# A hybrid encoder layer: state fetches moved a step forward, bias rows spread head by head, transposes at the top, and another row buffer

## The chip, the cores and the metric

The kernel runs on one core of a Trainium2 chip. The metric is the device time of one execution in microseconds, as the median of several runs. A core has five engines with queues of their own: TensorE (PE; its weight loads are listed as PEld), VectorE (DVE), ScalarE (ACT), GpSimd (POOL) and SyncE (SP). SP computes nothing here; it issues most of the transfers. Some transfers of results are issued on ACT's queue. Each queue is worked off in order, and an instruction that waits holds up those behind it on its engine.

## The reference

One layer of a hybrid encoder, for a prompt of 2048 rows and for a sample of 8 streams of 16 rows, all in float32 with a model width of 1024:

```python
h = rms_norm(x, norm_g[0]); z = h @ w_in                  # 1024 -> 3592, columns split among heads
att = band_attention(qa, ka, va, rel_table)               # 8 heads of 64, own 64-row chunk + 8 before, clipped relative bias
hb, (c1, n1, m1) = mlstm_sequence(qb, kb, vb, ig, lf, ..) # 4 heads of 128, matrix memory c, gates, running maximum
mix = concat(rms_norm(att), headnorm(hb) * g_mlstm * sigmoid(ob)) @ w_out
x = x + rms_norm(mix, norm_g[1])
u = rms_norm(x, norm_g[2]) @ w_up                         # 1024 -> 2 * 2816
y = b_conv + sum(ext[:, j:j + S] * w_conv[j] for j in range(3))   # causal, along the rows
x = x + rms_norm((gelu(gate) * up) @ w_down, norm_g[3])
```

For the sample, attention also reads a cache of 512 keys and values per stream, the mLSTM starts from given states (`state_c`, one matrix of 128 x 129 for each of 4 heads and 8 streams, the normaliser in its first column), and the convolution has its own two rows of history. Besides both outputs the layer returns new keys, values, states and convolution histories.

## The kernel before

**Precision.** Each float32 operand of a large product is split into a high and a low part, and a product is made of three matmuls (`mm3`, L93 to L97): high by high, high by low, low by high. The split is a cast on ACT and a subtraction on DVE.

**Part one, projection with attention and mLSTM** (about 0 to 1200 us). The rows are taken in two halves, and in each half 14 groups of columns of `w_in` follow one another: for each group TensorE multiplies the transposed, normed rows with the group's weights, which arrive in raw tiles `wi_raw` (L1155) and are split at L1161 and L1162. `norm_tile` (L209) norms 128 rows and turns them with eight transposes into `hT`. Two other streams of work run between these matmuls, each as a `Pipe` (L135): attention (`att_stream`) and the mLSTM (`mem_stream`). A pipe holds small generators, "units". Each call of `step` takes a new unit from its source and moves every unit in it on by one `yield`; a unit's first stage usually issues its loads, the next splits, the next multiplies. `pump` (L171) steps the two pipes in turn, by a running estimate of TensorE and DVE time that each `yield` carries.

**The order of the queues.** The program text gives the priorities. A planner then simulates all the engines and takes, whenever one is free, the earliest instruction of the program that could run, so a load may be put ahead of others that stand before it, as far as its buffer is free. A transfer inside `tc.keep_in_program_order` keeps its place. The order so found is fixed in the queues.

**The bias.** The attention bias depends on the distance of query and key alone. `build_bias` (L285) loads the reversed table (`near`, L290), negates it and fills the far side (L292, L293), writes both to a DRAM row `ext` of 767 numbers for each head, and then copies each head's row 128 times to `relrow` (L298, 383.5 KB a head). `load_head` (L315) reads a 128 x 640 tile `nb` out of `relrow` with rows one shorter than the step, which gives the diagonal pattern. Its unit is the first of the attention pipe. On the other pipe run, at the same time, `prep_sample` and `prep_prompt` (L541), which make the stabilised gates: cumulated sums, a running maximum `cm` (a scan on DVE at L548), transposes `rt`, `mp` and `pkT`, exponentials on ACT (L570 to L573).

**The sample's states.** `mlstm_sample` handles one head for the eight streams. Its units are `own`, four `batches` (L759) of two streams each, and `finish`. A batch loads two states into `cs` (L763), makes masked queries and values (POOL and DVE), multiplies (L775, L776), updates the states (L779, L780) and stores them (L781). `cs` shares two buffers, tag `num`, with the results of the prompt's mLSTM chunks, which `finish_heads` stores at L649.

**Part two, output projection** (`project`, L956, to about 1340 us), with the third part's rows being prepared beside it.

**Part three, the FFN** (to the end). It takes the rows in three blocks of about 700. For a block, the normed rows are turned and combined into seven operands `B[0]` to `B[6]` of a Strassen-like scheme (`h2_units`, L1051; one tile each, 128 x 2 x 4 x 384). For each of 22 column groups the up projection runs seven products, the convolution makes `y` rows on ACT and DVE, and the gated result `g` is stored to DRAM in `gd`. Then the down projection reads `gd` back, tile by tile (`fetch`, L1438, with the load at L1447), splits it and multiplies. While it runs, the next block's `h2_units` are stepped. `row` (L1044) hands out the 128 x 1024 row tiles of tag `yq`, three buffers: they hold `y` and `g` in the up projection, the fetched `gr` in the down projection, the rows `x2r` of the first block, and the squares `sq`, an output nobody reads, which ACT writes at L1069 while it sums them.

Of the kernel before, what the change touches and what calls it, by code (L numbers as in the profile page):

```python
# [44 lines left out]
def hymba_step(ctx: ExitStack, tc: tile.TileContext, I: dict, O: dict):  # L45
# [27 lines left out]
    make_identity(nc, ident)  # L73
    nhalf = const.tile([P, 8], F32, name="nhalf")
    nc.vector.memset(nhalf, -0.5)

    def mean_square(ms, ssq, n, eps=EPS):
        nc.gpsimd.tensor_scalar(ms, ssq, 1.0 / n, eps, op0=ALU.mult, op1=ALU.add)
# [203 lines left out]
    def raw_tile(name):  # L282
        return pa.tile([P, LS], F32, tag="raw", name=name, bufs=3)

    def build_bias():  # L285
        ext = dt_([HA, SQ], "ext")

        def unit():
            far, near = raw_tile("relf")[:HA, :383], raw_tile("reln")[:HA, :SQ - 383]
            tc.keep_in_program_order(nc.sync.dma_start(near, I["rel_rev"][:, 0:SQ - 383]))  # L290
            yield 0.0, 0.0
            nc.vector.tensor_scalar(near, near, -1.0, None, op0=ALU.mult)  # L292
            nc.vector.tensor_copy(far, near[:, 0:1].broadcast_to([HA, 383]))  # L293
            nc.sync.dma_start(ext[:, 383:SQ], near)
            nc.sync.dma_start(ext[:, 0:383], far)
            yield 0.0, 0.75
            for h in range(HA):
                nc.sync.dma_start(relrow[h], ext[h:h + 1, :].broadcast_to([P, SQ]))  # L298
                yield 0.0, 0.0

        yield unit()
        yield FLUSH
# [12 lines left out]
    def load_head(s):  # L315
        pair, kg, hh, h, nm = s.pair, s.kg, s.hh, s.h, s.nm
        if kg % 2 == 0:
            nb = pa.tile([P, 640], F32, tag="nb", name=f"nb{nm}", bufs=2)
            nc.sync.dma_start(nb, bias_src(h, P, 640))
            nc.gpsimd.memset(nb[0:64, 576:640], BIG)  # L320
            nc.gpsimd.memset(nb[64:128, 0:64], BIG)
            nbs[hh] = nb
        s.nb = nbs[hh]
        rows = slice(hh * 64, hh * 64 + 64)
        qr = raw_tile(f"qraw{nm}")[:, :512]
        krs = [raw_tile(f"kraw{nm}_{g}")[:, :512] for g in s.segs]
        for r in range(2):
            nc.sync.dma_start(qr[r * 64:r * 64 + 64, :], qTd[pair][kg][rows, :])
        for kr, g in zip(krs, s.segs):
            for r in range(2):  # L330
                nc.sync.dma_start(kr[r * 64:r * 64 + 64, :], kTd[pair][g][rows, :])
        yield 0.0, 0.0
        s.kh = pa.tile([P, 1024], F32R, tag="kh", name=f"kh{nm}", bufs=2)
        s.kl = pa.tile([P, 1024], F32R, tag="kl", name=f"kl{nm}", bufs=2)
        s.qs = pa.tile([P, 512], F32R, tag="qs", name=f"qs{nm}", bufs=2)
        nc.scalar.copy(s.qs, qr)
        nc.vector.tensor_tensor(s.qs[64:128], qr[64:128], s.qs[64:128], op=ALU.subtract)
        for si, kr in enumerate(krs):
            c = slice(si * 512, (si + 1) * 512)
            nc.scalar.copy(s.kh[:, c], kr)  # L340
            nc.vector.tensor_tensor(s.kl[:, c], kr, s.kh[:, c], op=ALU.subtract)
        new = [g for g in s.segs if g == kg or (h, g) not in vhl]
        vrs = [raw_tile(f"vraw{nm}_{g}")[:, :4 * DA].rearrange("p (a d) -> p a d", a=4) for g in new]
        for vr, g in zip(vrs, new):
            nc.sync.dma_start(vr, vd[h // 4][g][:, :, (h % 4) * DA:(h % 4 + 1) * DA])
        yield 0.0, 0.6 + 0.6 * len(krs)
        for vr, g in zip(vrs, new):
            t = pa.tile([P, 4, P], F32R, tag="vhl", name=f"vhl{nm}_{g}", bufs=4)
            nc.scalar.copy(t[:, :, 0:DA], vr)
            nc.vector.tensor_tensor(t[:, :, DA:P], vr, t[:, :, 0:DA], op=ALU.subtract)  # L350
            vhl[h, g] = t
        s.v = {g: vhl[h, g] for g in s.segs}
        if kg % 2:
            for g in s.segs:
                vhl.pop((h, g))
        yield 0.0, 0.34 * len(new)
# [294 lines left out]
    def mlstm(h, half):  # L651
# [22 lines left out]
        def chunk(s, c):  # L674
            cc = 2 * s.pc + c
            r = cc * HB + h
            col = lambda i: cols[:, i, r:r + 1]
            q_, k_ = s.qk[:, 0, c * P:(c + 1) * P], s.qk[:, 1, c * P:(c + 1) * P]
            sp = ps_sm(f"ms{s.nm}_{c}")
            nc.tensor.matmul(sp[:, 0:P], k_, q_, start=True, stop=True)  # L680
            transpose(sp[:, P:2 * P], k_)
            w = pm.tile([P, P], F32, tag="wexp", name=f"w{s.nm}_{c}", bufs=2)
            nc.scalar.activation(w, s.mb[:, c, :], AF.Exp, bias=col(0), scale=-1.0)
            kw = pm.tile([P, P], F32, tag="kw", name=f"kw{s.nm}_{c}", bufs=2)
            nc.scalar.activation(kw, sp[:, P:2 * P], AF.Identity, scale=col(3))
            nc.vector.tensor_tensor(w, sp[:, 0:P], w, op=ALU.mult)
            yield 0.32, 0.2
            if c == 0:
                s.num = pm.tile([P, 2, e], F32, tag="num", name=f"num{s.nm}", bufs=2)
            num = s.num  # L690
            acc = ps_sm(f"ma{s.nm}_{c}")
            nc.tensor.matmul(acc[:, e:2 * e], q_, cst[h], start=True, stop=True)
            nc.tensor.matmul(acc[:, 0:e], w, s.va[:, c, :], start=True, stop=True)
            nc.tensor.matmul(acc[:, 2 * e:3 * e], kw, s.va[:, c, :], start=True, stop=True)
            nc.vector.scalar_tensor_tensor(cst[h], cst[h], dec[:, cc, h:h + 1], acc[:, 2 * e:3 * e],
                                           op0=ALU.mult, op1=ALU.add)
            nc.scalar.activation(num[:, c, :], acc[:, e:2 * e], AF.Identity, scale=col(1))
            nc.vector.tensor_tensor(num[:, c, :], num[:, c, :], acc[:, 0:e], op=ALU.add)
            yield 0.65, 0.47
            if c == 0:  # L700
                return
            r0 = 2 * s.pc * HB + h
            sg, o = s.t0 // 4, s.t0 % 4
            finish_heads(num, cols[:, 2, r0:r0 + HB + 1:HB], s.og, h, 2,
                         mixd[sg][:, o:o + 2, 512 + h * DH:512 + (h + 1) * DH], s.nm)
            if half == 1 and s.pc == 3:
                nc.sync.dma_start(O["c_prompt"][h], cst[h])
            yield 0.0, 1.3
# [11 lines left out]
    def mlstm_sample(h):  # L720
# [36 lines left out]
            yield 0.2, 0.2  # L757

        def batches(bp):  # L759
            yield 0.0, 0.0  # L760
            bs = slice(2 * bp, 2 * bp + 2)
            cs = pm.tile([P, 2, e], F32, tag="num", name=f"cs{h}_{bp}", bufs=2)
            nc.sync.dma_start(cs, I["state_c"][h][:, bs])  # L763
            qz = pm.tile([P, 2, P], F32, tag="mqk", name=f"qz{h}_{bp}", bufs=2)
            nc.gpsimd.memset(qz, 0.0)
            for i in range(2):
                c = slice((2 * bp + i) * DS, (2 * bp + i + 1) * DS)
                nc.gpsimd.tensor_copy(qz[:, i, c], s.qt[:, c])
            vz = pm.tile([P, 2, e], F32, tag="mvo", name=f"vz{h}_{bp}", bufs=2)
            nc.vector.tensor_tensor(vz, s.va.unsqueeze(1).broadcast_to([P, 2, e]),  # L770
                                    ind[:, bs].unsqueeze(2).broadcast_to([P, 2, e]), op=ALU.mult)
            yield 0.0, 0.3
            cu = ps_sm(f"cu{nm}_{bp}")
            for i in range(2):
                nc.tensor.matmul(cu[:, 2 * e:3 * e], qz[:, i, :], cs[:, i, :], start=(i == 0), stop=(i == 1))  # L775
            nc.tensor.matmul(cu[:, :2 * e], s.kw, vz.rearrange("p b e -> p (b e)"), start=True, stop=True)  # L776
            nc.vector.scalar_tensor_tensor(s.num[:, 0, :], cu[:, 2 * e:3 * e], col(1), s.num[:, 0, :],
                                           op0=ALU.mult, op1=ALU.add)
            nc.vector.tensor_tensor(cs, cs, dec[:, h, bs].unsqueeze(2).broadcast_to([P, 2, e]), op=ALU.mult)  # L779
            nc.vector.tensor_tensor(cs, cs, cu[:, :2 * e].rearrange("p (b e) -> p b e", b=2), op=ALU.add)  # L780
            nc.sync.dma_start(O["c_sample"][h][:, bs], cs)  # L781
            yield 0.85, 0.8
# [259 lines left out]
        return ffn.p3.tile([P, 512], F32, tag="q", name=name, bufs=11)  # L1042

    def row(name):  # L1044
        return ffn.p3.tile([P, D], F32, tag="yq", name=name, bufs=3)

    def new_B(i, b):
        pool = ffn.p3 if i < EARLY_B else ffn.p4
# [2 lines left out]
    def h2_units(b, between=()):  # L1051
# [3 lines left out]
        def unit(halves, col, n, nm):  # L1055
# [10 lines left out]
            rs = {}  # L1066
            for t, x in rows_.items():
                ssq = small.tile([P, 1], F32, tag="ssq", name=f"fssq{t}")
                nc.scalar.activation(row(f"sq{t}"), x, AF.Square, accum_out=ssq)  # L1069
                rs[t] = rsqrt_mean(ssq, D, f"n2_{t}")  # L1070
            yield 0.0, 0.0
            for t, x in rows_.items():
# [606 lines left out]
```

## Time and profile before

| | |
|---|---|
| median of 3 runs | 2814.91 us |
| lowest, highest | 2813.02, 2816.5 us |
| the profiled execution | 2812.18 us |
| its span, first to last instruction | 2810.5 us |
| mean granted TensorE clock | 0.997 |

A line of a timeline is: start in us, length in us, engine, line of the kernel, operation, what it writes and reads, and in brackets how long the engine had been idle and what ended the idle time. SPq and ACTq are transfers as their queue issues them; the length is that of the issue, not of the transfer. A line of the waits is: who waited, for whom, total us, times, longest. A line of the windows gives the busy time of each engine in one stretch, then the clock that TensorE was granted there, the share in which the DMA engines were busy, and GB/s.

### The profile page before, as it was taken

The numbers are of one execution on the slowest core, as the hardware profiler recorded it, in microseconds if no ns is written. First come the engines' busy times: TensorE is split into PE (matmuls) and PEld (weight loads), VectorE is DVE, ScalarE is ACT, GpSimd is POOL, SyncE is SP. The second block draws the span as 40 slices with busy tenths as digits, with TensorE's granted clock in tenths as the row PEclk, the third lists the DMA queues.
The fourth block names the chain that finished last, engine by engine and source line by source line (L and its number), as shares of the span: only waits on it lengthen the run. The fifth ranks groups of instructions, "written<-read, shape, count | busy, mean of one in ns | idle before, by whom it ended". The sixth has DMA issues, their size and how long they took to land.

```text
span 2810.5 us, 47049 instructions
## 1 busy us (share of the span) xinstructions
PE 2729.8 (97%) x16587; PEld 2550.2 (91%) x16587; DVE 1871.9 (67%) x3442; ACT 1407.5 (50%) x2836; POOL 446.2 (16%) x876
## 2 busy tenths in 40 slices
PE   8899999999999999999999999999999999999998
PEld 7899999998899998878999988799999878999887
DVE  5344455646446678666989886457878854888855
ACT  4345545644356666543545555445555543555533
POOL 1000010211100003244221110011111310222221
PEclk9999999999999999999999999999999999999999
DMA  4544355557555455355645455644544775555585
GB/s 164 170 128 125 111 155 156 177 148 215 164 173 148 141 177 172 106 180 203 199 160 173 162 177 172 218 145 154 157 154 139 266 264 155 171 181 175 188 298 197
DMA packets 313418, 486.04 MB, mean 173 GB/s; under 512 B 55426, under 2 KB 150622, under 8 KB 313054
## 3 DMA queue, kind: packets, MB, share of 16 engines
q1 hardware_dynamic: 274590, 449.21, 50.9%
q10 hardware_dynamic: 38592, 33.83, 3.6%
q8 instruction: 130, 2.13, 0.3%
q14 instruction: 106, 0.87, 0.1%
HBM read 359.36 MB, written 126.70 MB: 173 GB/s over the span
## 4 chain that ended last, share of the span: by engine, by line
PE 51%; DVE 5%; DMA 2%; issue 2%; ACT 1%; POOL 1%; SPq 0%; DVEq 0%; POOLq 0%; ACTq 0%
PE uec L95 5%; PE uec L96 5%; PE uec L97 5%; PE dn L96 4%; PE dn L97 4%; PE dn L95 4%; PE ua L97 3%; PE ua L96 3%; PE ua L95 3%; PE dnm L95 2%; PE dnm L97 2%; PE dnm L96 2%; PE wo L95 1%; PE wo L97 1%; PE wo L96 1%
## 5 line engine op out<-in xcount | busy, mean ns | idle before, releaser
L95 PE MATMUL uec<-B,wuh 128*128 128x384 f32 (+1 forms) x720 | 236.3, 329 | 6.9 <-DVE uu L1492 6.1
L96 PE MATMUL uec<-B,wuh 128*128 128x384 f32 (+1 forms) x720 | 235.2, 327 | 0.0
L97 PE MATMUL uec<-B,wul 128*128 128x384 f32 (+1 forms) x720 | 233.3, 327 | 0.0
L1251 DVE TENSOR_TENSOR gl<-gr,gh 128x768 fp32r<-128x768 f32 (+3 forms) x141 | 118.7, 849 | 163.3 <-ACT gh L1250 163.0
L1250 ACT CAST gh<-gr 128x768 fp32r<-128x768 f32 (+3 forms) x141 | 102.1, 736 | 219.1 <-PE dn L96 194.1
L1250 ACT CAST wuh<-wu 128x512 fp32r<-128x512 f32 x255 | 141.7, 617 | 91.2 <-PE uec L96 87.5
L95 PE MATMUL dn<-wdh,gh 128*128 128x512 f32 x466 | 182.9, 392 | 2.5 <-DVE ug L1403 2.5
L96 PE MATMUL dn<-wdl,gh 128*128 128x512 f32 x466 | 183.9, 395 | 0.0
L97 PE MATMUL dn<-wdh,gl 128*128 128x512 f32 x466 | 168.4, 396 | 0.0
L1251 DVE TENSOR_TENSOR wul<-wu,wuh 128x512 fp32r<-128x512 f32 x255 | 164.3, 683 | 2.8 <-DMA x2d<-mx 2.8
L96 PE MATMUL vo<-wi_l,hT 128*128 128x256 f32 x544 | 155.7, 286 | 0.0
L95 PE MATMUL vo<-wi_h,hT 128*128 128x256 f32 x544 | 154.9, 285 | 0.6 <-DVE mt L199 0.6
L97 PE MATMUL vo<-wi_h,hT 128*128 128x256 f32 x544 | 155.3, 285 | 0.0
L387 DVE CUSTOM_DVE_ANT_0 tmp<-s,nb 128x640 f32<-128x640 f32 (+4 forms) x128 | 94.3, 737 | 77.8 <-PE s L377 74.3
L95 PEld LDWEIGHTS uec<-B,wuh 128*128 128x128 f32 x720 | 135.1, 188 | 11.1 <-DVE uu L1492 8.1
L96 PEld LDWEIGHTS uec<-B,wuh 128*128 128x128 f32 x720 | 135.2, 188 | 0.1
L97 PEld LDWEIGHTS uec<-B,wul 128*128 128x128 f32 x720 | 135.0, 188 | 0.0
L388 ACT ACTIVATE tmp<-tmp,mn 128x640 f32<-128x640 f32 (+4 forms) x128 | 97.6, 762 | 69.9 <-DVE mn L387 65.6
L95 PE MATMUL qk<-hT,wi_h 128*128 128x384 f32 (+1 forms) x384 | 128.6, 335 | 3.5 <-ACT qk_st L226 1.7
L400 DVE TENSOR_TENSOR ptl<-pt,pth 128x640 fp32r<-128x640 f32 (+4 forms) x128 | 93.5, 737 | 55.4 <-ACT pth L399 54.4
L97 PE MATMUL qk<-hT,wi_l 128*128 128x384 f32 (+1 forms) x384 | 128.0, 333 | 0.0
L96 PE MATMUL qk<-hT,wi_h 128*128 128x384 f32 (+1 forms) x384 | 127.8, 333 | 0.0
(409 smaller groups left out, 8886.6 us busy)
## 6 DMA issues: line engine op xcount, KB each, us to landing
wu<-in_w_up SPq DMA_DIRECT2D x220, 256.0 KB, 4.0
wu<-wsd SPq DMA_DIRECT2D x176, 256.0 KB, 3.7
wdr<-in_w_down SPq DMA_DIRECT2D x132, 256.0 KB, 5.4
gr<-gd SPq DMA_DIRECT2D x78, 384.0 KB, 3.9
wi_raw<-in_w_in SPq DMA_DIRECT2D x52, 512.0 KB, 4.3
wsd<-ws SPq DMA_DIRECT2D x88, 256.0 KB, 4.0
gd<-g SPq DMA_DIRECT2D x44, 384.0 KB, 2.7
kraw<-kTd SPq DMA_DIRECT2D x112, 128.0 KB, 3.2
```

The costliest lines, as they stand in the source:

```text
L95: nc.tensor.matmul(out, ah, bh, start=start, stop=False, skip_group_check=onto)
L96: nc.tensor.matmul(out, ah, bl, start=False, stop=False, skip_group_check=onto)
L97: nc.tensor.matmul(out, al, bh, start=False, stop=stop, skip_group_check=onto)
L387: nc.vector.tensor_tensor_reduce(o_, s_, b_, 1.0, 3e38, ALU.add, ALU.min, accum_out=mn)
L388: nc.scalar.activation(tmp[:, :n], tmp[:, :n], AF.Exp, bias=mn, scale=-1.0, accum_out=rsum[:, i % 4, hh:hh + 1])
L400: nc.vector.tensor_tensor(s.ptl[:, sl, qc], ptv, s.pth[:, sl, qc], op=ALU.subtract)
L1250: nc.scalar.copy(h, r)
L1251: nc.vector.tensor_tensor(l, r, h, op=ALU.subtract)
```

## The change

Five edits:

1. At the top, 28 transposes of the identity matrix into a PSUM tile that nothing reads.
2. `build_bias` lets three more steps pass between the load of the table and its use. It spreads the rows of heads 0 and 1 alone. The row of head h + 2 is spread when head h is loaded for the first time, and these copies keep their place in the program.
3. `batches` allocates and loads `cs` ahead of its first `yield` in place of behind it, and the tag `num` gets a third buffer.
4. The squares of full 128-row tiles go into the part of `B[0]` that the same unit overwrites two stages later; those of the half tiles of the last block still go to a row tile.
5. The tag `yq` gets a fourth buffer.

```diff
+    warm = ps_sm("warm")
+    for _ in range(28):
+        transpose(warm[:, :P], ident)
...
+    ext = dt_([HA, SQ], "ext")
+
+    def spread_bias(h):
+        tc.keep_in_program_order(nc.sync.dma_start(relrow[h], ext[h:h + 1, :].broadcast_to([P, SQ])))
+
     def build_bias():
-        ext = dt_([HA, SQ], "ext")
 
         def unit():
             far, near = raw_tile("relf")[:HA, :383], raw_tile("reln")[:HA, :SQ - 383]
             tc.keep_in_program_order(nc.sync.dma_start(near, I["rel_rev"][:, 0:SQ - 383]))
-            yield 0.0, 0.0
+            for _ in range(4):
+                yield 0.0, 0.0
...
-            for h in range(HA):
-                nc.sync.dma_start(relrow[h], ext[h:h + 1, :].broadcast_to([P, SQ]))
+            for h in range(2):
+                spread_bias(h)
                 yield 0.0, 0.0
...
             vhl[h, g] = t
+        if s.kg == 0 and h + 2 < HA:
+            spread_bias(h + 2)
...
-                s.num = pm.tile([P, 2, e], F32, tag="num", name=f"num{s.nm}", bufs=2)
+                s.num = pm.tile([P, 2, e], F32, tag="num", name=f"num{s.nm}", bufs=3)
...
         def batches(bp):
+            bs = slice(2 * bp, 2 * bp + 2)
+            cs = pm.tile([P, 2, e], F32, tag="num", name=f"cs{h}_{bp}", bufs=3)
+            nc.sync.dma_start(cs, I["state_c"][h][:, bs])
             yield 0.0, 0.0
-            bs = slice(2 * bp, 2 * bp + 2)
-            cs = pm.tile([P, 2, e], F32, tag="num", name=f"cs{h}_{bp}", bufs=2)
-            nc.sync.dma_start(cs, I["state_c"][h][:, bs])
...
     def row(name):
-        return ffn.p3.tile([P, D], F32, tag="yq", name=name, bufs=3)
+        return ffn.p3.tile([P, D], F32, tag="yq", name=name, bufs=4)
...
                 ssq = small.tile([P, 1], F32, tag="ssq", name=f"fssq{t}")
-                nc.scalar.activation(row(f"sq{t}"), x, AF.Square, accum_out=ssq)
+                if n == P:
+                    out, x = ffn.B[0][:, :, :, col:col + n], x.rearrange("p (a k c) -> p a k c", a=2, k=4)
+                else:
+                    out = row(f"sq{t}")
+                nc.scalar.activation(out, x, AF.Square, accum_out=ssq)
```

## The prediction

> **What bounds the kernel now.** I read the page first (shares by engine), then the waits of TensorE, then the windows at full and half clock, then the timelines of the four places where TensorE waits and the change reaches.
>
> ```profile
> span 2810.5 us, 47049 instructions
> PE 2729.8 (97%) x16587; PEld 2550.2 (91%) x16587; DVE 1871.9 (67%) x3442; ACT 1407.5 (50%) x2836; POOL 446.2 (16%) x876
> ```
> TensorE bounds it: 97% busy, the next engine 67%. Its idle time is 2810.5 - 2729.8 = 80.7 us. No part of the change takes a needed matmul away, so all that can be won is a share of these 80.7 us and of the time at half clock. The waits of TensorE (total us, times, longest):
>
> ```profile
> PE hT_pt L67 <- DVE xr L219: 10.0, 4, 8.2
> PE cus L775 <- DMA cs<-in_state_c: 8.4, 6, 2.5
> PE dnm L95 <- ACT gh L1250: 7.0, 5, 2.8
> PE uec L95 <- DVE uu L1492: 6.1, 6, 1.8
> PE pkTp L67 <- ACT pk L573: 4.8, 1, 4.8
> PE rt L67 <- DVE cm L548: 2.7, 1, 2.7
> ```
> The second, third, fifth and sixth rows belong to edits of the change, 22.9 us together; the first is the start. The fourth belongs to none: there DVE is the late one, and no DVE work goes.
>
> An idle stretch costs a second time, through the clock. These windows (PE, PEld, DVE, ACT, POOL busy, then PEclk, DMA share, GB/s) are cut where the granted clock changes:
>
> ```profile
> 95.87:99.29 3.42, 3.32 (x10) 3.02 (x11) 0.29 (x1) 1.12 (x4) 0.29 (x2) 0.50 0.60 196
> 713.69:717.10 3.41, 0.95 (x8) 0.78 (x8) 2.58 (x6) 1.12 (x3) 0.00 (x0) 1.00 0.43 103
> 717.10:720.51 3.41, 3.41 (x16) 3.22 (x15) 2.35 (x9) 0.83 (x2) 0.64 (x3) 0.50 0.49 164
> 1225.69:1229.10 3.41, 3.00 (x13) 2.60 (x14) 2.80 (x6) 1.24 (x2) 2.01 (x4) 0.50 0.33 78
> 1229.10:1232.50 3.40, 3.40 (x14) 2.48 (x15) 3.40 (x5) 3.38 (x7) 1.93 (x3) 1.00 0.84 290
> 2669.52:2672.94 3.42, 3.42 (x9) 2.66 (x9) 2.60 (x4) 0.72 (x1) 1.82 (x2) 0.50 1.05 407
> ```
> Four of them ran at 0.50, and each costs 3.41 x 0.5 = 1.7 us of work. Each lies behind a wait of TensorE; ahead of the one at 717.10 it was busy 0.95 of 3.41 us, 28%. So a wait that empties a stretch that far carries 1.7 us on top.
>
> **The change, part by part.**
>
> *Bias rows.* The eight copies that spread a bias row over 128 rows come at once, behind the table they are made from:
>
> ```profile
> 78.56 0.35 DVE L292 TENSOR_SCALAR reln<-reln 8x384 f32<-8x384 f32 x1 [8.91 <-DMA reln<-in_rel_rev]
> 79.92 0.41 DVE L548 TENSOR_TENSOR_SCAN cm<-ap 32x128 f32<-32x128 f32 x1
> 80.92 7.93 SPq L298 DMA_DIRECT2D relrow<-ext  x8
> 94.74 0.40 ACT L570 ACTIVATE pk<-cm,mprev 32x128 f32<-32x128 f32 x1 [9.06 <-DMA relrow<-ext]
> 106.94 1.14 ACT L1161 CAST wi_h<-wi_raw 128x512 fp32r<-128x512 f32 x2 [1.99 <-DMA wi_raw<-in_w_in]
> ...
> relrow<-ext SPq DMA_DIRECT2D x8, 383.5 KB, 8.4
> ```
> Two losses. VectorE waits 8.91 us for the table at L292, in order, and the scan L548 queued behind it is what TensorE waits 2.7 us for. Then the copies, 8 x 383.5 KB, hold the SP queue 7.93 us, take 8.4 us to land, and hold ScalarE 9.06 us at L570; the transpose pkTp behind it is the 4.8 us wait, and 1.7 us of clock follow. Together 2.7 + 4.8 + 1.7 = 9.2 us. In the changed kernel VectorE's two instructions come three steps later, behind the scan, and two copies are issued here instead of eight (2 of 7.93 / 8 = 1.0 us each on SP). What is late next is the weight load wi_raw: ScalarE still waits for it at 106.94, and TensorE arrives 2.7 + 4.8 = 7.5 us sooner. That load is issued on SP behind the copies too, so it comes earlier, but not by all of it. I keep 7.0 of 9.2 us; the ends are 2 (only the table's wait goes) and 9.2.
>
> The other six copies move to the loading of heads 0 to 5, each two heads ahead of its use, 1.0 us of SP each. Nothing waits in them: their source is long written. They fall in a stretch with room:
>
> ```profile
> 160.00:200.00 40.00, 40.00 (x264) 39.77 (x264) 16.81 (x36) 18.33 (x41) 0.58 (x4) 1.00 0.40 122
> ```
> DMA is at 0.40 and TensorE full, so I cost them at nothing. Without that cover one copy held a queue for 9.06 us at worst; that is a rival below.
>
> *State fetches.* Each head's sample takes its states in four batches. The load of a batch needs one of two num buffers, and a buffer is free only when its old content has been stored:
>
> ```profile
> SPq L763 <- DMA out_c_sample<-cs: 21.4, 7, 4.5
> ...
> 709.74 0.34 SPq L781 DMA_DIRECT2D out_c_sample<-cs  x1
> 714.30 0.33 SPq L763 DMA_DIRECT2D cs<-in_state_c  x1
> 714.72 0.39 SPq L891 DMA_DIRECT2D svr<-in_cache_v  x1
> 719.53 0.33 SPq L763 DMA_DIRECT2D cs<-in_state_c  x1
> ```
> The load at 714.30 stood behind the landing of the store at 709.74, held up the cache load at 714.72, and arrived just too late: TensorE waited 2.5 us, the longest of the six, and the clock fell at 717.10. With a third buffer, and the load a step earlier, the same load needs no store; the one after it needs the store of 709.74 and has a whole further batch. Loads are 719.53 - 714.30 = 5.2 us apart at the closest, against waits of at most 2.5, so one batch of lead covers every one. That gives 8.4 + 1.7 = 10.1 us. Late next are the cache loads that share SP, like the one at 714.72, so I keep 8.0; the ends are 0 and 10.1. The DVE and POOL work of a batch is the same as before.
>
> *Idle transposes.* Eight transposes take 1.97 us at the start and 1.09 us later:
>
> ```profile
> 1.35 0.28 POOL masks.py:199 TENSOR_SCALAR_AFFINE_SELECT ident<-ident 128x128 f32<-128x128 f32 x1
> 8.17 1.97 PE L67 MATMUL hT_pt<-ident,xr 128*128 128x128 f32 x8 [8.17 <-DVE xr L219]
> 10.68 0.99 ACT L198 CAST hT<-hT_pt 128x1024 fp32r<-128x1024 f32 x1
> 16.59 1.32 DVE L1162 TENSOR_TENSOR wi_l<-wi_raw,wi_h 128x528 fp32r<-128x528 f32 x2
> 17.26 1.09 PE L67 MATMUL hT_pt<-ident,xr 128*128 128x128 f32 x8
> ...
> 41.23 1.06 ACT L216 ACTIVATE hT<-xr 128x1024 fp32r<-128x1024 f32 x1 [4.17 <-DMA xr<-in_x_sample]
> ```
> They can start at 1.63 and last 28 x 1.97 / 8 = 6.9 us if all are slow, to 8.5: at worst 0.4 us beyond 8.17. At best TensorE is at full clock from 8.17. But the first cast, at 10.68, follows other ScalarE work, not the transposes; the gaps of the start stay and may send the clock down again; and at 16.59 the low half of the next weights comes from VectorE, its first half done 1.32 / 2 = 0.66 us later, at 17.3; TensorE takes it now behind the transposes that end at 17.26 + 1.09 = 18.35. So it is 1.0 us at most there, and part of that goes at 41.23, where a DMA is the late one. I take 0.5; ends -0.4 and 1.0.
>
> [...]
>
> ```profile
> 1225.85 1.97 PE L67 MATMUL mT_pt<-ident,mr 128*128 128x128 f32 x8 [3.04 <-DVE mr L979]
> 1227.62 1.06 PE L1081 MATMUL h2T_pt<-ident,x2r 128*128 128x128 f32 x4
> ```
> The half-clock stretch 1225.69 to 1229.10 held almost nothing but these twelve transposes, and the clock was back at 1.00 right behind it.
>
> *Scrap of squares and row buffer.* In the fetch loop of the down projection the row buffers are short:
>
> ```profile
> SPq L1447 <- DVE gl L1251: 188.6, 72, 4.4
> SPq L1447 <- ACT sq L1069: 10.7, 6, 2.6
> ...
> 2657.88 0.32 SPq L1503 DMA_DIRECT2D gd<-g  x1
> 2658.25 0.42 SPq L1447 DMA_DIRECT2D gr<-gd  x1
> 2662.27 0.46 SPq L1447 DMA_DIRECT2D gr<-gd  x1
> 2668.23 0.72 ACT L1250 CAST gh<-gr 128x640 fp32r<-128x640 f32 x1 [0.28 <-DMA gr<-gd]
> ```
> A fetch waits on SP until a row is split, or a scrap of squares is done with. At the last block's switch the first fetch went out at 2658.25, only after the last product had been stored from its row; the next, at 2662.27, landed at 2668.2, and TensorE waited 2.8 us with 1.7 us of clock behind. A fourth row lets both go one place earlier. That is 2.8 + 1.7 = 4.5 us. DMA is full there (1.05 in the window from 2669.52), so what is fetched early displaces something: I keep 3.5; ends 0 and 4.5. The other waits of dnm, 7.0 - 2.8 = 4.2 us, I leave. The squares cost the same on ScalarE wherever they go. At the opening of the FFN, units of block 0 get their rows a unit ahead, but TensorE's wait at 1225.85 hangs on the first unit's load: nothing.
>
> **Sum.** 7.0 + 8.0 + 0.5 + 3.5 = 19.0 us. One cost no row shows: the order within each queue is planned anew. It could add or remove one wait like those above, 2.8 + 1.7 = 4.5 us; I take 0 and keep both ends. The profiled execution took 2812.2 us (1.7 around its span); 2812.2 - 19.0 = 2793.2. The median of the runs, 2814.9, lies 2.7 above: 2795.9, so **2796**.
>
> **The rivals.**
> - *The wait moves to the neighbours on SP, or to the weights.* If state loads still block SP, cache loads take over the wait (8.0 lost, 2804); if wi_raw at 106.94 hardly moves, 5.0 of the first term go (2801); both 2809. For: both rows are there, beside the ones removed. Against: SP waits there because of the buffers that are added.
> - *Nothing measurable.* New order costs 4.5, and two terms fall to their low ends (-5.0, -8.0): 2796 + 17.5 = 2813.5. For: every term is a few us. Against: four independent places.
> - *Slower.* The six moved copies each hold a queue as the eight did. Price 4.8 + 1.7 = 6.5 us each, 39 us in all, 2796 + 39 = 2835; from the third on (19.5 us) the gain is gone. For: ScalarE has been held 9.06 us by just these copies. Against: there eight came within 7.93 us; where the six go, DMA stands at 0.40.
> - *The change misses its aim*: the planner hoists loads anyway, so "one step earlier" says nothing. It is the first rival for the state loads; the third buffer acts regardless.
>
> **How the numbers follow.** Forecast (2788 to 2800) 0.55; more than forecast, with all terms at their upper ends (24.8 us, 5.8 more) and one wait less (4.5), 2786, 0.05; first rival (2800 to 2809) 0.23; nothing measurable 0.12; slower 0.05. About 0.2%, 5.6 us, is what a measurement of this kernel can tell from no change: 2809.3 to 2820.5. Faster 0.83, same 0.12, slower 0.05. The range takes the forecast and most of the first rival: 2787 to 2809.
>
> **What would show it.** Right: no wait of cus for cs; no 4.8 us gap before pkTp and the clock at 1.00 around 96 and 717; relrow copies spread out to some 350 us; the gap at 2669 gone. Wrong: waits of ss or sot for skh or svh grown by several us between 400 and 750; waits of qk or va for weight casts near 100; ScalarE held by relrow copies later; new half-clock stretches.

## The result and the profile after

| | before | after |
|---|---|---|
| median | 2813.25 us (5 runs, 2808.23 to 2816.50) | 2831.46 us (5 runs, 2823.68 to 2833.62) |
| ratio | | 1.0057, interval 1.0038 to 1.0077 |
| the profiled execution | 2812.18 us | 2832.0 us |
| mean granted clock | 0.997 | 0.990 |

The change makes the kernel 0.57% slower; 2796 us was forecast, and the range ended at 2809. Lines of the changed kernel stand 4 to 15 higher than before: L1081 is L1096 now, L979 is L990.

The head of the page after:

```profile
span 2830.2 us, 47096 instructions
PE 2747.1 (97%) x16615; PEld 2565.9 (91%) x16615; DVE 1876.7 (66%) x3442; ACT 1408.5 (50%) x2836; POOL 426.6 (15%) x876
```

TensorE's idle time is 2830.2 - 2747.1 = 83.1 us, against 80.7 before: 2.4 us more. Its busy time grew by 17.3 us. The 28 new transposes account for 4.9 of them; the other 12.4 us are the old matmuls, run slower. So between these two executions the waits won and lost nearly cancel and a slower clock is left, which a list of waits alone would not show. One caution: 67 other executions of before have a mean clock of 0.9956, so the profiled one, at 0.997, is some 4 us better off than usual (0.0014 x 2810; an estimate). The waits of TensorE after (total us, times, longest):

```profile
PE mT_pt L67 <- DVE mr L990: 8.6, 6, 2.7
PE pt L67 <- ACT tmp L399: 7.3, 3, 4.1
PE h2T_pt L1096 <- DVE x2r L1088: 7.1, 3, 5.7
PE ss L99 <- ACT skh L857: 5.3, 3, 3.8
```

The wait for `cs` is gone, that of `pkTp` for `pk` too: both aims are met. In their place stand four others that were 3.0, 2.1, 1.6 and 1.9 us before. Nearly all of the wait of `h2T_pt` and 3.4 us of that of `mT_pt` lie around 1240 us, where output projection and FFN meet, a place that no edit touches directly; the other 5.2 us of `mT_pt` lie in the projection ahead of it.

**Where the time is lost.** Matmul by matmul, in the order in which they ran and without the new transposes, after stands against before at about +8 us at 900 us, at +28.5 us from 1250 to 1350 us, and at +19.7 us at the end. So some 20 us arise at the end of part one and some 9 us are won back in the FFN. The windows of both kernels from the first matmul of the output projection to the first of the up projection, cut at the last attention matmul and at the first transpose of the FFN's opening (PE, PEld, DVE, ACT, POOL busy, PEclk, DMA share, GB/s); before:

```profile
1055.50:1207.60 152.10, 148.25 (x867) 127.34 (x866) 113.31 (x222) 85.24 (x218) 45.41 (x67) 1.00 0.44 135
1207.60:1219.50 11.90, 11.85 (x51) 9.21 (x50) 3.45 (x5) 4.36 (x10) 1.79 (x4) 1.00 0.57 168
1219.50:1329.10 109.60, 104.37 (x496) 84.78 (x497) 75.46 (x75) 41.72 (x87) 52.55 (x62) 0.98 0.58 193
```

After:

```profile
1054.90:1232.50 177.60, 165.83 (x952) 140.37 (x952) 124.74 (x251) 96.18 (x245) 47.31 (x75) 0.99 0.42 131
1232.50:1243.80 11.30, 5.64 (x25) 4.20 (x23) 3.36 (x5) 4.65 (x11) 1.75 (x4) 0.87 0.78 255
1243.80:1357.60 113.80, 107.49 (x497) 86.95 (x498) 74.61 (x74) 41.22 (x85) 52.33 (x63) 0.94 0.53 177
```

The three stretches last 273.6 us before and 302.7 after, 29.1 us more. Idle time is 9.1 and 23.7 us (length less PE busy, summed): 14.6 more. At half clock are 3.4 us before, 20.5 after: 17.1 x 0.5 = 8.5 more. The remaining 6 us are 60 more matmul records (1474 against 1414), work of attention and mLSTM that before has done ahead of the projection.

Two rows changed. In the first, idle time grew from 3.9 to 11.8 us, in small waits of the projection (`mT_pt` for `mr`, 5.2 us in four; `wo`, 3.9 us in six); no experiment below takes these apart. The second row is the place where the stages meet, and it is the one to look at closely. The last attention matmul is followed by some 12 us of other things before the FFN's first rows are ready, in both kernels. Before, 51 records fill them to 11.85 us of 11.90; after, 25 records fill 5.64 of 11.30. The timeline of that place, before (`ao` is the last attention matmul, `x2r` the FFN's rows):

```profile
1207.18 0.38 PE L67 MATMUL ao<-ident,attT 128*128 128x128 f32 x2
1209.59 13.57 SPq L1061 DMA_DIRECT2D x2r<-x2d  x4
1215.98 1.06 ACT L1069 ACTIVATE sq<-x2r 128x1024 f32<-128x1024 f32 x1 [0.60 <-DMA x2r<-x2d]
1219.51 0.63 PE L1081 MATMUL h2T_pt<-ident,x2r 128*128 128x128 f32 x4
```

After:

```profile
1232.16 0.38 PE L67 MATMUL ao<-ident,attT 128*128 128x128 f32 x2
1234.58 13.87 SPq L1072 DMA_DIRECT2D x2r<-x2d  x5
1240.40 1.06 ACT L1084 ACTIVATE B<-x2r 128x1024 fp32r<-128x1024 f32 x1 [0.71 <-DMA x2r<-x2d]
1243.83 1.12 PE L1096 MATMUL h2T_pt<-ident,x2r 128*128 128x128 f32 x4 [5.69 <-DVE x2r L1088]
1253.44 1.97 PE L67 MATMUL mT_pt<-ident,mr 128*128 128x128 f32 x8 [2.66 <-DVE mr L990]
```

From `ao` to the first `h2T_pt` it is 12.3 us before, 11.7 after. By the program, the row tiles of the FFN lie in space that part one gives back when its last attention work is done (`open_ffn`), so by this reading the chain (load, squares, norm) cannot begin earlier; from `ao` on it took 11.7 to 12.4 us in the six kernels read at this place (before, after, the state part alone, the load kept in order, two buffers, the fill). What differs is what lies beside it. In after the granted clock fell to 0.50 behind a window with TensorE busy for 0.78 of 3.42 us; windows of after:

```profile
1237.36:1240.78 3.42, 0.78 (x4) 0.30 (x2) 0.69 (x1) 1.10 (x3) 0.00 (x0) 1.00 0.96 335
1240.78:1244.19 3.41, 0.36 (x2) 0.36 (x3) 1.28 (x1) 3.22 (x9) 1.85 (x5) 0.50 0.74 303
...
1247.60:1251.02 3.42, 2.46 (x11) 1.66 (x9) 1.97 (x3) 1.05 (x3) 3.18 (x6) 0.50 0.49 159
...
1254.43:1257.84 3.41, 3.41 (x13) 2.62 (x11) 3.41 (x3) 1.50 (x2) 3.41 (x2) 0.50 0.98 233
```

From 1240.78 to 1257.84 the clock stays at 0.50: five windows, where before had one (1225.69 to 1229.10).

### The profile page after: what moved, and what is told of

Same layout as the page of the kernel before. It is cut to its first block, busy times and chain, and to the rows that moved or that the text cites. A ratio compares the mean times of both kernels' runs of the same rounds, so it can differ in the third digit from the quotient of the medians.

```text
span 2830.2 us, 47096 instructions
## 1 busy us (share of the span) xinstructions
PE 2747.1 (97%) x16615; PEld 2565.9 (91%) x16615; DVE 1876.7 (66%) x3442; ACT 1408.5 (50%) x2836; POOL 426.6 (15%) x876
## 4 chain that ended last, share of the span: by engine, by line
PE 77%; DMA 10%; DVE 6%; issue 3%; ACT 2%; POOL 1%; SPq 0%; ACTq 0%; DVEq 0%; POOLq 0%
PE uec L99 6%; PE uec L100 6%; PE uec L101 6%; PE dn L101 4%; PE dn L100 4%; PE dn L99 4%; PE ua L101 3%; PE ua L100 3%; PE ua L99 3%; PE dnm L101 2%; PE dnm L99 2%; PE dnm L100 2%; PE qb L101 2%; PE qb L99 2%; PE qb L100 2%
```

## The experiments

Each ratio is to the kernel before, run on the same chip beside it (its median there was 2809.3 to 2809.5 us); the interval is 95%.

**First the four parts, each alone** (edits 1, 2, 3, and 4 with 5 of the change).

> The kernel before with the 28 idle transposes alone; every queue keeps its order behind them. Theory (the clock gate as the changed kernel's trace shows it): the clock rises at about 5 us, falls again in the gap ahead of the first products and is half until about 18 us, so the start gains nothing and may lose: 0 to +4 us against before. Rival (my prediction): -0.5 us, and no half-clock stretch between 8 and 20 us.

> The kernel before with the bias rows spread per head alone. Theory: the 4.8 us wait before pkTp goes, the wait for the scan stays in part, and a new wait of 2 to 4 us comes behind the mLSTM's row loads near 100 us; the output projection keeps its cover: -5 to 0 us. Rival 1 (my prediction): -7 us. Rival 2 (the moved copies are what made the whole change slower): +10 us or more, with ScalarE or TensorE held between 100 and 350 us.

> The kernel before with the state fetch a step earlier and three num buffers alone. Theory: the waits of cus for cs go, but the planner's order from there on is another one; at the opening of the FFN only half as much output projection is left behind the last attention work, so TensorE waits some 6 to 10 us there with half clock behind: +8 to +18 us. Rival 1 (my prediction): -8 us. Rival 2 (the changed kernel's loss is a matter of the edits together, or of the row buffer): within 4 us of before.

> The kernel before with the squares in B[0] and the fourth row buffer alone. Theory: the queues are the same up to the output projection, the cover there stays, and the FFN from its first up projection on gains as it did in the changed kernel: -5 to -9 us. Rival 1 (the fourth x2r load and the squares' wait for B[0] make the loss at the opening of the FFN): +5 to +15 us, with TensorE waiting over 4 us for the first x2r. Rival 2 (my prediction): -3.5 us, all of it at the last block's switch.

| part | median, us | ratio | interval |
|---|---|---|---|
| idle transposes | 2815.23 | 1.0019 | 1.0009 to 1.0029 |
| bias rows | 2809.66 | 1.0002 | 0.9992 to 1.0011 |
| state fetches | 2833.17 | 1.0083 | 1.0068 to 1.0098 |
| squares and fourth row | 2803.54 | 0.9982 | 0.9971 to 0.9993 |

The whole loss is in the state fetches, from which 8 us of gain were forecast. At 23.9 us it is also more than the 8 to 18 expected from the meeting place alone. Its four executions have a mean clock of 0.9922, the 24 of before beside them 0.9955: so some 9 of the 23.9 us are clock (0.0078 x 2831 - 0.0045 x 2808; an estimate). Its profile has the same picture at the opening of the FFN:

```profile
1226.62 0.38 PE L67 MATMUL ao<-ident,attT 128*128 128x128 f32 x2
1238.88 1.12 PE L1081 MATMUL h2T_pt<-ident,x2r 128*128 128x128 f32 x4 [6.31 <-DVE x2r L1073]
1250.47 1.97 PE L67 MATMUL mT_pt<-ident,mr 128*128 128x128 f32 x8 [4.62 <-DVE mr L979]
```

and 20.5 us at half clock from 1235.3 on. The edit moves a load in the middle of part one. That it costs time some hundreds of us later speaks for the order of the queues, which is planned for the whole program. TensorE's order is that of before up to 464 us and another one from there on. Which half of the edit does it? With two buffers the move does nothing: two kernels further down, the whole change with two buffers and the one without the idle transposes, differ in the place of this load and in these transposes alone, and TensorE ran the other 16587 matmuls in the same order in both. That the third buffer changes the order with the load at its old place too was read from the queues as built; no run shows it, and what the runs show is the third buffer together with the moved load. In that order, behind the projection's first matmul stand 355 matmul records of attention in place of 316, and ahead of the FFN's opening 24 of the projection in place of 51.

**Then the order against the buffer.** The third buffer and the moved load, but the load kept in program order:

```diff
+            cs = pm.tile([P, 2, e], F32, tag="num", name=f"cs{h}_{bp}", bufs=3)
+            tc.keep_in_program_order(nc.sync.dma_start(cs, I["state_c"][h][:, bs]))
+            yield 0.0, 0.0
```

> The state part of the change with one word more: the load of the carried state stands a step earlier and has the third buffer, as in the state-alone kernel (2833.17 us, +23.9 on its before), but the load is kept in program order. In the built queues TensorE then again has 51 matmul records of the output projection between the last attention matmul and the first transpose of the FFN's opening (state alone 24), and 316 attention records behind the first of the projection (state alone 355), as the kernel before has. Theory A, the loss is the order that the planner lays once the third buffer lets it, above all the thin cover at the opening of the FFN: about the kernel before, ratio 0.997 to 1.002, and no stretch at half clock longer than 7 us between 1200 and 1260 us. Rival B, the third buffer or the earlier load itself costs (space, transfers, a wait of its reader), whatever the order is: ratio 1.005 to 1.009 again.

2809.41 us, ratio 0.9997 (0.9985 to 1.0009); between 1200 and 1260 us the clock is down for one window of 3.4 us. Theory A: the third buffer costs nothing by itself. The order is not that of before everywhere (TensorE's departs from it at 415 us), but the meeting place again has its 51 records. Its profiled execution is the slowest of the twelve, 2818.91 us. Its TensorE group reads:

```profile
L775 PE MATMUL cus<-cs,qz 128*128 128x129 f32 x64 | 10.3, 283 | 0.0
```

The 0.0 is the idle time ahead of it, 8.4 us before. So this run is also the test of the state term with its side effect taken away: the wait is wholly gone, and nothing is won. In its place stand these groups, which had 1.1 and 4.0 us before:

```profile
L680 PE MATMUL ms<-mqk 128*128 128x128 f32 x128 | 25.5, 281 | 4.8 <-DVE w L686 3.5 <-DMA mqk<-qkbd 1.0 <-DVE num L698 0.2
L67 PE MATMUL pt<-ident,tmp 128*128 128x128 f32 x560 | 84.4, 274 | 6.3 <-DVE ptl L400 3.6 <-ACT tmp L388 2.5
```

**The whole change with two buffers.**

```diff
-                s.num = pm.tile([P, 2, e], F32, tag="num", name=f"num{s.nm}", bufs=3)
+                s.num = pm.tile([P, 2, e], F32, tag="num", name=f"num{s.nm}", bufs=2)
...
-            cs = pm.tile([P, 2, e], F32, tag="num", name=f"cs{h}_{bp}", bufs=3)
+            cs = pm.tile([P, 2, e], F32, tag="num", name=f"cs{h}_{bp}", bufs=2)
```

> The whole change with only the number of the num buffers put back from 3 to 2; the load still stands before its step's yield, the transposes, the bias rows and both FFN edits stay. Theory A, the third buffer carries the whole loss by the order that it brings, and the other parts are what they were alone (transposes +0.19%, bias rows 0, FFN edits -0.18%): ratio 0.998 to 1.002, time 2805 to 2815 us, 51 projection records as cover. Rival B, the loss comes from the moved load or from the parts together: ratio 1.004 or more.

2799.87 us, ratio 0.9968 (0.9955 to 0.9982), a little better than either theory had it. One number taken back, 3 to 2, turns +0.57% into -0.32%: 0.89% of 2809.5, 25 us. The opening of the FFN is as before:

```profile
1204.50:1216.30 11.80, 11.80 (x53) 9.42 (x52) 3.45 (x5) 4.36 (x10) 2.07 (x6) 1.00 0.68 254
```

**The halves of the FFN edit.**

> The fourth row buffer of the FFN alone; the squares still go to a row of the same ring. The two FFN edits together gave ratio 0.9982 [0.9971, 0.9993]. Theory A, the gain is the ring being one deeper, so that output rows wait less: ratio 0.997 to 0.999. Rival B, the gain is that the squares leave the ring: ratio 0.9995 to 1.0005 here, and the whole gain in the squares-alone run.

> The scrap of the squares into the buffer of the transposed rows alone; the ring stays at three rows. Theory A (the gain is the deeper ring): ratio 0.9995 to 1.0005 here. Rival B (the squares held a row): ratio 0.997 to 0.999. If both halves give it, each alone is enough to free the row that was missing.

The fourth row alone: 2801.56 us, 0.9969 (0.9958 to 0.9980). The squares alone: 2810.95 us, 1.0003 (0.9993 to 1.0014). The gain is the deeper ring, and it lies elsewhere than forecast. The up projection's group before, and with the fourth row:

```profile
L95 PE MATMUL uec<-B,wuh 128*128 128x384 f32 (+1 forms) x720 | 236.3, 329 | 6.9 <-DVE uu L1492 6.1 <-DVE uu L1403 0.8
```

```profile
L95 PE MATMUL uec<-B,wuh 128*128 128x384 f32 (+1 forms) x720 | 235.0, 328 | 1.3 <-DVE uu L1403 0.9 <-DVE uu L1492 0.3
```

What ACT's first step of the convolution (L1422, which takes a row for `y`) waited for, before:

```profile
  DVE uu L1492: 56.4, 22
  DVE g L1498: 30.4, 17
  DVE g L1501: 8.4, 8
```

`g` is the product that lets a `y` row go: 25 waits for a row buffer. With four rows both `g` rows are gone from this list. ACT started late; DVE's next step on that row (L1423) waited 22.2 us for it before and 10.2 with four rows; DVE's `uu` stood behind that step in DVE's queue, and TensorE waited for `uu`. All twelve profiles agree: TensorE's wait for `uu` at this line (L1492 of before) is 4.5 to 6.2 us in the seven kernels with three rows, the squares-alone kernel among them, and at most 0.8 in the five with four. The wait that was to go, `dnm` at the last block's switch, did not: the gap there is 3.8 us, against 2.8 before. But the smaller waits of `dnm` for `gh` did, 4.2 us which the forecast had left alone.

Both edits together gave 0.9982, a little less than the row alone; the intervals overlap, so whether the squares take something back is open.

**The opening's gap filled with idle work.** The state part alone, with

```diff
+            if late and col == 0:
+                fill = ps_sm("fill")
+                for _ in range(60):
+                    tc.keep_in_program_order(nc.tensor.transpose(fill[:, :P], ident, ident))
```

> The state part alone, as in the state-alone kernel (2833.17 us, ratio 1.0083 [1.0068, 1.0098]), and 60 idle transposes of the identity beside the opening of the FFN; in the built queue they stand right behind the last attention matmul, ahead of the 24 remaining records of the projection, so that some 6 to 7 us more work lies between that matmul and the first transpose of the opening, whose rows come some 12 us after it. They compute nothing that is used. Theory A, the loss there is wait and clock together: the row's gap of 6.31 us shrinks below 1.5 us, the stretch at half clock behind it falls from 20.5 us to 10.3 us or less, and the time falls by half of what that stretch loses, 3 to 8 us: ratio 1.0055 to 1.0075. Rival B, the loss is the lateness of the attention work alone, and the clock drops there for the later gaps whatever is put ahead: stretch and time as before, ratio 1.008 or more. Rival C, the fill fails to hide anything and costs its own 6 to 7 us: ratio 1.010.

2827.64 us, ratio 1.0059 (1.0044 to 1.0074), 5.5 us below the state part alone, as theory A has it, though the two intervals still overlap:

```profile
1224.94 0.38 PE L67 MATMUL ao<-ident,attT 128*128 128x128 f32 x2
1225.16 6.71 PE L1078 MATMUL fill<-ident 128*128 128x128 f32 x60
1237.32 0.60 PE L1085 MATMUL h2T_pt<-ident,x2r 128*128 128x128 f32 x4
```

The 6.31 us gap ahead of `h2T_pt` is filled, and the half clock behind falls from 20.5 to 6.8 us (1241.5 to 1248.3), which is worth 13.7 x 0.5 = 6.8 us. The fill takes 6.7 us of TensorE itself where it would have waited, and no useful work came earlier: from `ao` to `h2T_pt` it is still 12 us. So here some 6 us of the loss are clock. The mean clock of all its executions says the same: 0.9945 against 0.9922, 0.0023 x 2830 = 6.5 us. The rest, some 18 us, no run divides: there are the waits of this order in the projection (the first row of the windows above), and what clock is lost elsewhere.

**Without the idle transposes.** The two-buffer version less edit 1 (and with the load back at its place, which leaves the queues as they are).

> The kernel of the two-buffer run (ratio 0.9968 [0.9955, 0.9982]) less the 28 idle transposes at the top: bias rows per head and both FFN edits, the state part wholly taken out (in the built queues the moved load with two buffers stands where it stood before, so only the transposes differ). Theory A, the idle transposes cost what they cost alone (+0.19% [0.09, 0.29]): ratio 0.994 to 0.996, below 2799 us. Rival B, that cost was a matter of where that one build's waits met the clock's windows and is not there in this build: ratio 0.9965 to 0.998, as in the two-buffer run or in the run of the fourth row alone.

2803.15 us, ratio 0.9973 (0.9961 to 0.9984). Rival B: in this build the transposes cost nothing that can be seen (0.9968 with them, and the intervals overlap), though alone they cost 0.19%.

**A version that beats both.** The fourth row alone (0.9969), or the whole change with two buffers (0.9968); no run separates them. Of the five edits, the gain is in one.

## Why the prediction was wrong, point by point

**The step that failed** is the last of the sum: "the order within each queue is planned anew. It could add or remove one wait like those above, 2.8 + 1.7 = 4.5 us; I take 0 and keep both ends." The term was named and mis-sized. The runs show +25 us (0.9968 against 1.0057), not within 4.5. Between the change forecast, -19.0 us, and the one measured, +16.0 (0.57% of 2813), lie 35 us: 25 are this order, and 10 are the terms below, which without it brought 9.0 in place of 19.0. The bound came from the waits that were there. But a new order can open a place that shows no wait at all because it is just covered, and the second row of the windows of before was such a place: 11.85 us of cover for a chain of 11.9. The prediction did not look for it. It is not the whole of the 25 us: there are 5.6 us of new idle time in that row and most of the half clock behind it, but also 7.9 us more idle in the row ahead. The size of the parts stays open; that they come with the order is shown by the two runs that take the order back, 0.9997 and 0.9968.

**State fetches, 8.0 us expected.** The wait goes as forecast; the gain is 0. The 8.4 us were themselves a high reading of one execution: in the profiles of four other kernels whose TensorE order is that of before up to 1230 us (idle transposes, both row edits, each row edit alone) the same wait is 6.5, 4.1, 5.0 and 4.9 us. In the run with the order kept the ratio is 0.9997 (-4.2 to +2.5 us). What is late next was put at the cache loads for 2.1 us; in that run it was the mLSTM's `w` and attention's `ptl`. The fourth rival was half right. "One step earlier" says nothing with two buffers; "the third buffer acts regardless" was true, but it acted through the planner.

**Bias rows, 7.0 us expected.** The gain is 0 (1.0002, 0.9992 to 1.0011). Rows of after:

```profile
81.21 0.35 DVE L301 TENSOR_SCALAR reln<-reln 8x384 f32<-8x384 f32 x1 [8.85 <-DMA reln<-in_rel_rev]
82.57 0.41 DVE L559 TENSOR_TENSOR_SCAN cm<-ap 32x128 f32<-32x128 f32 x1
106.06 0.90 POOL L678 TENSOR_SCALAR_AFFINE_SELECT mb<-mb 128x256 f32<-128x256 f32 x2 [12.55 <-DMA mb<-md]
106.51 0.40 ACT L694 ACTIVATE w<-mb,colsp 128x128 f32<-128x128 f32 x1 [5.56 <-POOL mb L678]
108.04 0.47 PE L67 MATMUL pt<-ident,tmp 128*128 128x128 f32 x1 [4.12 <-ACT tmp L399]
```

The table's wait is as long as before and still ahead of the scan: three more steps in the program did not move it in DVE's queue. The wait of `pkTp` did go, but at 108.04 TensorE waits 4.12 us ahead of attention's `pt`: ACT was held by POOL's mask, and that by the load of `mb`. Neither that load nor this wait was among the forecast's neighbours. It grows with the edit: `pt` waits 4.1 to 7.3 us for `tmp` in the four kernels with the bias part, 1.2 to 4.2 in the others.

**Idle transposes, 0.5 us expected.** Alone +0.19%, 5 us slower, a little more than the 0 to 4 expected of that run; in the version without the third buffer nothing. The forecast that the clock may fall again at the start was right:

```profile
1.74:5.15 3.41, 3.41 (x16) 3.41 (x17) 0.00 (x0) 1.28 (x2) 0.81 (x5) 1.00 0.77 260
8.56:11.98 3.42, 0.75 (x7) 0.51 (x5) 1.33 (x2) 3.21 (x6) 0.71 (x2) 1.00 1.06 364
11.98:15.39 3.41, 2.81 (x12) 2.50 (x13) 3.34 (x4) 2.83 (x7) 1.60 (x5) 0.50 0.84 297
```

The clock, up at 5.15, is down again at 11.98 and up at 18.80; before it came up at 17.37. (The clock's records begin at 5.15 here and at 17.37 in before; the 1.00 of the first row only says that there is none yet.) Where the 5 us of the transposes-alone run come from is not settled. TensorE's order differs from before in these 28 instructions alone. Its profile is level with that of before at 50 us, 1.9 us ahead at 700 and 7.7 behind at the end, and between 20 and 2800 us it has 34.1 us at half clock against 13.7. But it is the slowest of its nine executions, 2819.83 us, and that of before has a better clock than most. Over all executions the mean clock is 0.9939 against 0.9955, 4.5 us, of which up to 3.4 are the half clock from 11.98 on, which the records of before do not cover.

**Rows, 3.5 us expected.** Right in sign, under half in size, wrong in place: 8.7 us (0.31% of 2809.5), from `uec` waiting for `uu` (5.6 us less idle in its group) and from the smaller waits of `dnm`. The prediction gave that wait away: "there DVE is the late one, and no DVE work goes." DVE was late because ACT, ahead of it, waited for a row of the ring that the change deepens.

**The rivals.** "Slower" by 39 us had its cause in the six moved copies; the part that holds them is at 1.0002, so they show no such cost. Slower came true by another mechanism. Two of the signs of being wrong that the prediction named are there: `ss` waits 5.3 us for `skh`, against 1.9, and there are new half-clock stretches.

## What to carry to other kernels

Where a planner fixes the queues, one more buffer is a new order for all that follows; compare the order of each edit alone before costing its waits, since here that shows which half of an edit is empty and where the order moves. In the profile, look for places where two stages meet and the cover is as long as the chain behind it: such a place shows no wait, and here it broke. Read a wait of a few us in more than one execution before it becomes a term. And when a wait goes away, count as won only what the next waiter leaves, and ask of every late engine what it waited for itself.

## What the runs showed of the hardware

- **Behind stretches of transposes the clock stood at 1.00.** The window 1.74 to 5.15 of after held 3.41 us of idle transposes of the identity and nothing else on TensorE; up to 5.16 they start 0.21 us apart, behind it 0.11, and the clock's first record, at 5.15, is 1.00. In before, TensorE was busy for 3.00 us of the half-clock stretch 1225.69 to 1229.10, all but 0.2 us of that with the transposes `mT_pt` and `h2T_pt`, and from 1229.10 on the clock was 1.00.
- **In after the clock stood at 0.50 through three full windows in a row.** They were full by busy times whose ends are modelled, and the clock was 1.00 again only behind the third:

```profile
745.84:749.26 3.42, 3.42 (x9) 2.32 (x9) 1.86 (x3) 1.24 (x3) 1.71 (x3) 0.50 0.44 137
749.26:752.67 3.41, 3.41 (x13) 2.75 (x13) 1.33 (x2) 1.19 (x3) 0.00 (x0) 0.50 0.55 199
752.67:756.08 3.41, 3.41 (x12) 3.41 (x12) 1.35 (x3) 1.07 (x2) 0.00 (x0) 0.50 0.59 164
```

  TensorE was busy 0.04 us in the window ahead of them. A wait of 3.8 us cost 10.2 us at half clock there, 5.1 us of work, and not 1.7 as the prediction priced each wait. The kernel with the load kept in order has the same picture: TensorE full at 0.50 from 642.49 to 652.73, behind a wait of 2.27 us. In both, three `sot` matmuls of 16 rows lie in the first two windows; the third of after holds none. In before, one window at 0.50, 717.10 to 720.51, was followed by 1.00. Why it took three windows here and one there is open.
